# A decoder trunk on one core: the second pass of each feed forward begins with its gate and up column as one pair made of seven products of quarters

## The chip, the core and the metric

The kernel runs on one core of a Trainium2 chip. The core has a matrix engine (PE, with its weight loads shown apart as PEld), a vector engine (DVE), an activation engine (ACT), GpSimd (POOL) and a sync engine (SP) that mostly starts DMAs. The metric is the device time of one execution in microseconds (us), the median of several runs.

## What is computed

A trunk of two layers over 512 tokens of width 1024: a gated DeltaNet mixer in the first, sliding-window attention in the second, both with four heads of attention into memory tokens, and a SwiGLU feed forward behind each mixer. The change touches the feed forwards alone:

```python
D_MODEL, SEQ, D_FF = 1024, 512, 2816

def swiglu(h, w_gate_up, w_down):
    gu = h @ w_gate_up
    return (jax.nn.silu(gu[..., :D_FF]) * gu[..., D_FF:]) @ w_down
...
        x = x + swiglu(rms_norm(x, ln_ffn[layer]), w_gate_up[layer], w_down[layer])
```

## The kernel before, in words

Activations lie with features on the 128 partitions and the 512 tokens along a row. The normed input of a feed forward is eight tiles of 128 features. Every float32 number that goes into a large product is split into a high part (`h`, `whi`) and a low part (`l`, `wlo`), and each product is three matmuls (`mm3`, L198): high by high, high by low, low by high. All go through `mm` and are shown as line L146. The split of a weight tile (`split`, L168) is one copy on ACT (L140, writes `whi`) and one subtraction on DVE (L153, writes `wlo`).

`ffn` (L1099) goes through the 22 column tiles of the hidden width in two passes of 11 (L1167). A pass makes 11 hidden tiles, and then the eight rows of the product with `w_down` add the pass's part to the residual `x`. The rows of the down product have matmuls into the bank `pj`, and their 22 weight splits come in two tiles of 768 and 640 columns for each row.

A column tile of gate or up is made in one of two ways.

- **A whole column** (`projected`, L210): eight tiles of 128 features by three matmuls, 24 matmuls of 128x512. Its weights come in one DMA of 512 KB and are split in one piece of 128x1024.
- **A pair of columns** (`begin`, L1139, with `quarters`, L1275): two columns together, as a product of a 2 by 2 matrix of quarters (which column, which half of the features) with a 2 by 2 matrix of quarters (which half of the features, which half of the tokens). Seven products of quarters stand for the eight, after Strassen and Winograd. Each product is four feature tiles by three matmuls of 128x256, so a pair takes 84 matmuls. On the activations' side the sums of quarters `t1` to `t4` are made once in a feed forward (`token_sums`, tiles `T`). On the weights' side the sums are made for every pair: two by DMAs that add onto a tile that a first DMA has filled (`ws`, L1283 on SP and L1286, L1287 on POOL), two by additions on DVE.

The seven products of a pair stand in this order: `11`, `t1`, `t2`, `21`, `22`, `t3`, `t4`. Three banks with the tag `g` hold them. The first two results are copied out by ACT (`held`, the tiles `fs`), then `t2` goes on top of the first in its bank, and that sum is copied out too. `t4` is the last, and it isn't run at once: `begin` puts it off until the next pair has run its products `11` and `t1`, and at the end of a pass the call of `end` (L1153) releases it.

Split weights of the quarters lie in a ring of six places (`ring`, L1130): three buffers `whi` and three `wlo`, of which each holds two places. Those are the same three buffers that the whole columns and the rows of the down product use. When a pass begins, the ring is laid out anew. The raw weights have two buffers of 1024 columns for whole rows of weights (`wraw`, from the pool of weights) and two of 512 for the last quarter of each pair (`wraw` too, L1289).

A pass begins with a gate and an up column as two whole columns, in both passes, and the other ten columns of gate and of up are pairs (in the first pass two more gate columns are whole, since the sums of tokens are made beside them). So before the change the second pass has two whole columns and ten pairs.

The order of each engine's instructions is set ahead by a scheduler in the framework, which puts DMAs and splits ahead of the code's order where it finds room. Each engine then takes its own list strictly in order (only weight loads overlap matmuls), and waits on semaphores where a row needs another engine's result. SP's and POOL's lists hold the DMA starts.

Of the kernel before, what the change touches and what calls it, by code (L numbers as in the profile page):

```python
# [9 lines left out]
F32 = mybir.dt.float32  # L10
F32R = mybir.dt.float32r
I32 = mybir.dt.int32
AF = mybir.ActivationFunctionType
ALU = mybir.AluOpType
# [4 lines left out]
P = 128  # L19
T = 512  # L20
# [66 lines left out]
class Builder:  # L87
# [1011 lines left out]
    def ffn(self, fp, xp, layer, h, apool, rope=False):  # L1099

        nc, a = self.nc, self.a
        acc = self.acc
        half = FT // 2
        acts, sums, open_pairs, places, waiting, shift, sized = [], [], [], [], [], [0], []

        col = lambda f, up: a["wgu"][layer, 2 * f + up]

        def gate(f, up=()):
            ps = self.project(col(f, 0), h, "pj")
            if f == 0:  # L1110
                list(zip(range(2), up))
                self.rstd_from(acc, *(self.t(fp, [P, T], F32R, "ws", 4) for _ in range(2)), after=self.last,
                               root=(self.cosT, self.sinT) if layer else None)
                self.use(SILU_SIN)
            g = self.t(fp, [P, T], F32, "fg", 4)
            self.tt(nc.vector, g, ps, self.rstd, ALU.mult)
            if f == 2:
                waiting.append(g)
            else:
                self.fn(g, g, AF.Silu)  # L1120
            return g

        def put(u):
            n = len(acts)
            if n == FT // 2 - 1 and not sized:
                sized.append(self.t(fp, [P, 40], F32, "rest"))
            acts.append(self.pair(apool) if n < KD else self.pair(fp, f"ac{n}"))
            self.split(u, *acts[-1])
# [10 lines left out]
        def begin(f, up, by, tag, bufs, then):  # L1139

            o = [self.t(fp, [P, T], F32, tag, bufs) for _ in range(2)]
            steps = self.quarters(fp, [col(f + i, up) for i in range(2)], sums, by, o, ring)
            shift[0] = P - 8
            next(steps)
            while waiting:
                x = waiting.pop()
                self.nosync(self.fn(x, x, AF.Silu), self.held)
            end()
            next(steps)
            open_pairs.append((steps, then, o))  # L1150
            return o

        def end():  # L1153
            if open_pairs:
                steps, then, o = open_pairs.pop()
                next(steps, None)
                for x in o:
                    then(x)

        def add(x, ps):  # L1160
            d = ps
            if not layer:
                d = self.t(fp, [P, T], F32, "fu", 3)
                self.tt(nc.vector, d, ps, self.rstd, ALU.mult)
            self.tt(nc.vector, x, d, x, ALU.add)

        for f0 in (0, half):  # L1167
            acts.clear()
            places.clear()
            up = self.projected(col(f0, 1), h, "g")  # L1170
            g = gate(f0, up)
            u = self.t(fp, [P, T], F32, "fu", 3)
            self.tt(nc.vector, u, list(up)[-1], g, ALU.mult)
            put(u)
            for f in range(f0 + 1, f0 + half, 2):
                if f == 1:
                    g = []
                    for i in range(2):
                        for _ in range(2 - i):
                            sums.append(self.token_sums(fp, layer, len(sums), h))  # L1180
                        g.append(gate(f + i))
                    sums.append(self.token_sums(fp, layer, len(sums), h))
                else:
                    g = begin(f, 0, (self.rstd, self.rstd), "fg", 4, lambda x: self.fn(x, x, AF.Silu))
                begin(f, 1, g, "fu", 3, put)
            end()
            self.acc = self.floor if layer else None
            tail = KD - 2 if f0 and layer else KD
            down = lambda m, j, n, **kw: self.weight(a["wdn"][layer, m][:, (f0 + j) * P:(f0 + j + n) * P], **kw)
            for m in range(tail):  # L1190
                if layer and f0 == 0:
                    self.tt(nc.vector, self.x[m], self.x[m], self.root, ALU.mult)
                ps = self.bank("pj")
                for j, n in ((0, 6), (6, 5)):
                    w = down(m, j, n)
                    for k in range(n):
                        self.mm3(ps, w, k, acts[j + k], j + k == 0, j + k == half - 1)
                add(self.x[m], ps)
                if f0:
                    self.acc = self.accumulate(xp, self.acc, self.x[m], m)  # L1200
                if rope and f0 == 0 and m == 0:
                    self.rope_tables(fp)
        if tail < KD:
# [31 lines left out]
            for n, (end, o) in enumerate(zip(ends, outs)):  # L1235
                self.store(*end, o, n)
# [35 lines left out]
        parts["21"], parts["22"] = ([x[:, i * q:(i + 1) * q] for x in h[j + 4]] for i in range(2))  # L1272
        return parts

    def quarters(self, fp, src, sums, by, u, ring):  # L1275

        nc = self.nc
        q = T // 2
        (a11, a12), (a21, a22) = ([c[:, :T], c[:, T:]] for c in src)
        a1 = self.load(src[0])  # L1280
        s1, s3 = (self.t(fp, [P, T], F32, "ws", 4) for _ in range(2))
        for to, part in ((s1, a21), (s3, a11)):
            ins = nc.sync.dma_start(to, part).ins  # L1283
            if self.behind is not None:
                self.nosync(ins, self.behind)
        nc.gpsimd.dma_start(s1, a22, accum_op=ALU.add)  # L1286
        nc.gpsimd.dma_start(s3, a21, accum_op=ALU.add)  # L1287
        last = self.t(fp, [P, T], F32, "wraw", 2)
        ins = nc.sync.dma_start(last, a22).ins  # L1289
        if self.behind is not None:  # L1290
            self.nosync(ins, self.behind)
        pa, pb, pc = (self.bank("g")[:, :q] for _ in range(3))

        def product(ps, raw, b, first):

            w = ring()
            self.split(raw, *w)
            for j in range(4):
                self.mm3(ps, w, j, sums[j][b], first and j == 0, j == 3, not first)

        def held(ps):
            o = self.t(fp, [P, q], F32, "fs", 3)
            self.copy(o, ps)
            return o

        product(pa, a1[:, :T], "11", True)
        p1 = held(pa)
        self.held = self.copied
        product(pc, s1, "t1", True)
        p5 = held(pc)  # L1310
        yield

        self.tt(nc.vector, a1[:, :T], s1, a1[:, :T], ALU.add)
        product(pa, a1[:, :T], "t2", False)
        u2 = held(pa)
        product(pb, a1[:, T:], "21", True)
        self.tt(nc.vector, u[0][:, :q], pb, p1, ALU.add)
        self.tt(nc.vector, a1[:, T:], a1[:, :T], a1[:, T:], ALU.add)
        product(pc, a1[:, T:], "22", False)
        self.tt(nc.vector, u[0][:, q:], pc, u2, ALU.add)  # L1320
        self.tt(nc.vector, u[0], u[0], by[0], ALU.mult)
        product(pa, s3, "t3", False)
        self.stt(u[1][:, q:], pa, -1.0, p5, ALU.mult, ALU.subtract)
        self.tt(nc.vector, u[1][:, q:], u[1][:, q:], by[1][:, q:], ALU.mult)
        yield
        product(pa, last, "t4", False)
        self.stt(u[1][:, :q], pa, -1.0, by[1][:, :q], ALU.mult, ALU.mult)
# [290 lines left out]
```

## Time and profile before

| | |
|---|---|
| median of 3 runs | 1130.86 us (1130.72 to 1131.07) |
| span of the profiled execution, first to last instruction | 1129.4 us |
| so around that span | about 1.5 us |
| PE / PEld / DVE / ACT / POOL busy | 1119.9 / 986.1 / 827.6 / 634.4 / 73.2 us |
| second pass, layer 0: two whole columns and ten pairs | about 466.7 to 577.0 us |
| second pass, layer 1: the same | about 949.8 to 1060.1 us |

The page gives one time of the profiled execution, its span; the runs' median lies 1.5 us above it, and that is taken as the part outside of the first and last instruction. Times of rows are microseconds from the span's start, a second number is a duration. The chain of waits lists in order of time what the end of the program depended on; a piece such as `x24` is so many instructions one behind another on one engine. A matmul's own duration in a timeline (0.39 us for 128x512) is longer than its distance to the next, because matmuls overlap; the distance is what counts on PE.

### The profile page before, as it was taken

How to read it: one execution, taken by the hardware profiler on the slowest of the kernel's cores; microseconds unless marked ns; L12 is line 12 of the kernel's file. 1: busy time of each engine (PE TensorE's matmuls, PEld its weight loads, DVE VectorE, ACT ScalarE, POOL GpSimd, SP SyncE). 2: the span in 40 equal slices, each digit the busy share in tenths (PEclk: the TensorE clock that was granted, in tenths of full speed). 3: DMA queues.
4: the chain of work that ended last, by engine and by line, in shares of the span. 5: the costliest groups of instructions: out<-in, count | busy, mean ns of one | idle time of the engine just before them, and what ended most of it. 6: DMA issues, size and time to landing. Idle time of an engine off the chain costs nothing.

```text
span 1129.4 us, 19330 instructions
## 1 busy us (share of the span) xinstructions
PE 1119.9 (99%) x7339; PEld 986.1 (87%) x7339; DVE 827.6 (73%) x1553; ACT 634.4 (56%) x1285; POOL 73.2 (6%) x91
## 2 busy tenths in 40 slices
PE   9999999999999999999999999999999999999997
PEld 8888778887899988899988887788999988999986
DVE  7676976577888975588955877839999634889643
ACT  8588664456566632366643555856666422666434
POOL 0000000000021001011000000000111000111001
PEclk9999999999999999999999999999999999999999
DMA  8344252234567536377533321116687533776232
GB/s 314 109 153 149 95 131 86 85 113 145 174 167 195 143 111 169 102 191 195 134 89 102 132 75 38 53 43 180 158 201 185 144 103 105 173 190 156 77 103 87
DMA packets 72401, 151.15 MB, mean 134 GB/s; under 512 B 16956, under 2 KB 18516, under 8 KB 72308
## 3 DMA queue, kind: packets, MB, share of 16 engines
q1 hardware_dynamic: 60884, 129.21, 36.3%
q0 software_dynamic: 11136, 20.45, 11.2%
q8 instruction: 57, 0.93, 0.3%
q14 instruction: 36, 0.29, 0.1%
q10 hardware_dynamic: 288, 0.26, 0.1%
HBM read 142.94 MB, written 6.96 MB: 133 GB/s over the span
## 4 chain that ended last, share of the span: by engine, by line
PE 96%; DVE 2%; ACT 1%; DMA 0%; issue 0%; DVEq 0%; SPq 0%; ACTq 0%
PE pj L146 46%; PE g L146 38%; PE sc L146 6%; PE qk L146 3%; PE pt L146 2%; PE pt L150 1%; PE g L150 1%; DVE big L153 1%; DVE qv L156 0%; DVE btmp L153 0%; DMA early<-in_early 0%; DVE wlo L153 0%; ACT sm L134 0%; DVE T L153 0%; DVE gcr L153 0%
## 5 line engine op out<-in xcount | busy, mean ns | idle before, releaser
L140 ACT ACTIVATE whi<-wraw 128x512 fp32r<-128x512 f32 (+3 forms) x318 | 235.3, 748 | 240.6 <-PE pj L146 164.0
L153 DVE TENSOR_TENSOR wlo<-wraw,whi 128x512 fp32r<-128x512 f32 (+3 forms) x318 | 262.8, 837 | 92.7 <-ACT whi L140 85.2
L146 PE MATMUL pj<-h,whi 128*128 128x512 f32 (+1 forms) x652 | 256.4, 395 | 0.0
L146 PE MATMUL pj<-l,whi 128*128 128x512 f32 (+1 forms) x652 | 254.4, 390 | 0.0
L146 PE MATMUL pj<-h,wlo 128*128 128x512 f32 (+1 forms) x652 | 254.0, 390 | 0.0
L146 PE MATMUL g<-T,whi 128*128 128x256 f32 x1216 | 216.8, 279 | 0.0
L146 PEld LDWEIGHTS g<-T,whi 128*128 128x128 f32 x1216 | 185.1, 188 | 1.3 <-DVE fu L156 1.3
L146 PE MATMUL g<-T,wlo 128*128 128x256 f32 x608 | 169.7, 279 | 0.0
L146 PEld LDWEIGHTS pj<-h,whi 128*128 128x128 f32 x652 | 122.4, 188 | 28.0 <-issue 4.1
L146 PEld LDWEIGHTS pj<-h,wlo 128*128 128x128 f32 x652 | 122.5, 188 | 25.4 <-issue 0.9
L146 PE MATMUL g<-l,whi 128*128 128x256 f32 (+1 forms) x500 | 144.5, 289 | 0.0
L146 PE MATMUL g<-h,whi 128*128 128x256 f32 (+1 forms) x500 | 144.4, 289 | 0.0
L146 PE MATMUL g<-h,wlo 128*128 128x256 f32 (+1 forms) x500 | 144.4, 289 | 0.0
L146 PEld LDWEIGHTS pj<-l,whi 128*128 128x128 f32 x652 | 122.6, 188 | 23.6 <-DVE l L1468 0.3
L146 PEld LDWEIGHTS g<-T,wlo 128*128 128x128 f32 x608 | 114.3, 188 | 0.0
L146 PEld LDWEIGHTS g<-h,whi 128*128 128x128 f32 x500 | 94.0, 188 | 1.9
L146 PEld LDWEIGHTS g<-l,whi 128*128 128x128 f32 x500 | 93.9, 188 | 1.9
L146 PEld LDWEIGHTS g<-h,wlo 128*128 128x128 f32 x500 | 93.9, 188 | 1.8
L1286 POOL DMA_DIRECT2D ws<-in_wgu x38 | 33.5, 881 | 733.0 <-DMA ws<-in_wgu 399.1
L140 ACT ACTIVATE whi<-ws 128x512 fp32r<-128x512 f32 x76 | 48.0, 631 | 42.0 <-PE g L146 35.6
L153 DVE TENSOR_TENSOR wlo<-ws,whi 128x512 fp32r<-128x512 f32 x76 | 52.0, 684 | 5.9 <-ACT whi L140 5.9
L1287 POOL DMA_DIRECT2D ws<-in_wgu x38 | 34.2, 900 | 196.4 <-DVE wlo L153 71.4
(421 smaller groups left out, 1683.2 us busy)
## 6 DMA issues: line engine op xcount, KB each, us to landing
wraw<-in_wgu SPq DMA_DIRECT2D x50, 512.0 KB, 4.4
ws<-in_wgu SPq DMA_DIRECT2D x76, 256.0 KB, 3.4
ws<-in_wgu POOLq DMA_DIRECT2D x76, 256.0 KB, 4.5
wraw<-in_win SPq DMA_DIRECT2D x26, 512.0 KB, 3.6
wraw<-in_wdn SPq DMA_DIRECT2D x32, 384.0 KB, 3.1
wraw<-in_wdn SPq DMA_DIRECT2D x32, 320.0 KB, 2.9
wraw<-in_wgu SPq DMA_DIRECT2D x38, 256.0 KB, 4.0
wraw<-in_wout SPq DMA_DIRECT2D x16, 512.0 KB, 3.6
```

The lines of the kernel that those rows point to most:

```text
L140: self.copied = self.nc.scalar.activation(out, in_, AF.Copy, **kw).ins
L146: return self.nc.tensor.matmul(out, lhsT, rhs, start=start, stop=stop, skip_group_check=more).ins
L150: return self.nc.tensor.transpose(out, in_, self.ident[:k, :k]).ins
L153: return eng.tensor_tensor(out=out, in0=a, in1=b, op=op).ins
L1286: nc.gpsimd.dma_start(s1, a22, accum_op=ALU.add)
L1287: nc.gpsimd.dma_start(s3, a21, accum_op=ALU.add)
```

## The change

The first gate column and the first up column of the second pass are no longer two whole columns. A new function `both` takes them as one pair through `quarters`: the pair's first column is the gate, its second the up column. The gate half is scaled by `rstd` as before and goes through SiLU in the middle of the pair (`then`), and the up half is multiplied by it. The first pass stays as it was.

```diff
+        def both(f):
+
+            o = [self.t(fp, [P, T], F32, *kind) for kind in (("fg", 4), ("fu", 3))]
+            steps = self.quarters(fp, [col(f, up) for up in range(2)], sums, (self.rstd, o[0]), o, ring,
+                                  lambda: self.fn(o[0], o[0], AF.Silu))
+            next(steps)
+            next(steps)
+            open_pairs.append((steps, put, o[1:]))
+
...
         for f0 in (0, half):
             acts.clear()
             places.clear()
-            up = self.projected(col(f0, 1), h, "g")
-            g = gate(f0, up)
-            u = self.t(fp, [P, T], F32, "fu", 3)
-            self.tt(nc.vector, u, list(up)[-1], g, ALU.mult)
-            put(u)
+            if f0:
+                both(f0)
+            else:
+                up = self.projected(col(f0, 1), h, "g")
+                g = gate(f0, up)
+                u = self.t(fp, [P, T], F32, "fu", 3)
+                self.tt(nc.vector, u, list(up)[-1], g, ALU.mult)
+                put(u)
...
-    def quarters(self, fp, src, sums, by, u, ring):
+    def quarters(self, fp, src, sums, by, u, ring, then=None):
...
         self.tt(nc.vector, u[0], u[0], by[0], ALU.mult)
+        if then is not None:
+            then()
         product(pa, s3, "t3", False)
```

In the lists of the engines this moves rows at two places of each second pass. The first is ACT's list where the first pass's down product ends and the second pass begins, in layer 0. `whi_839` is the last weight tile of the down product, `wraw_842` and `wraw_848` are the two whole columns, `wraw_856` the first pair. Before:

```order
L140 ACTIVATE whi_839_4876<-wraw_838_4874 128x640
L140 ACTIVATE whi_843_4900<-wraw_842_4898 128x1024
L140 ACTIVATE whi_849_4935<-wraw_848_4933 128x1024
L140 ACTIVATE whi_863_4984<-wraw_856_4971 128x512
L140 ACTIVATE whi_863_4984<-ws_857_4973 128x512
L140 ACTIVATE whi_865_4986<-wraw_856_4971 128x512 x2
L134 ACTIVATE fg_846_4929<-fg_846_4929 128x512
L140 ACTIVATE whi_867_4988<-wraw_856_4971 128x512
L140 ACTIVATE whi_867_4988<-ws_858_4974 128x512
L140 ACTIVATE h_852_4965<-fu_847_4932 128x512
L140 ACTIVATE whi_863_4984<-wraw_874_5089 128x512
L140 ACTIVATE fs_869_5004<-g_860_4981 128x256
```

And in the changed kernel, where `wraw_844`, `ws_845` and `ws_846` are the new pair and `wraw_862` is the pair behind it:

```order
L140 ACTIVATE whi_839_4876<-wraw_838_4874 128x640
L140 ACTIVATE whi_851_4913<-wraw_844_4900 128x512
L140 ACTIVATE whi_851_4913<-ws_845_4902 128x512
L140 ACTIVATE whi_853_4915<-wraw_844_4900 128x512 x2
L140 ACTIVATE whi_855_4917<-wraw_844_4900 128x512
L140 ACTIVATE whi_855_4917<-ws_846_4903 128x512
L140 ACTIVATE whi_851_4913<-wraw_862_5019 128x512
L140 ACTIVATE fs_857_4933<-g_848_4910 128x256
L140 ACTIVATE whi_851_4913<-ws_863_5021 128x512
```

The two copies of 128x1024 are gone, and the copies for six products of the new pair stand in one row behind the down product's last; the first copy out of a bank (`fs_857`) stands behind the first copy for the next pair (`whi_851` from `wraw_862`).

The second place is the end of the second pass. On PE, in layer 0, `pj` is the first row of the down product and `g` from `T_612` on is the last pair's put-off product `t4`. Before:

```order
L146 MATMUL g_990_6155<-T_637_3272,wlo_866_4987 128x256
L146 MATMUL pj_1000_6295<-h_852_4965,whi_1002_6298 128x512
L146 MATMUL pj_1000_6295<-l_853_4966,whi_1002_6298 128x512
L146 MATMUL pj_1000_6295<-h_852_4965,wlo_1003_6299 128x512
L146 MATMUL pj_1000_6295<-h_895_5278,whi_1002_6298 128x512
L146 MATMUL pj_1000_6295<-l_896_5279,whi_1002_6298 128x512
L146 MATMUL g_990_6155<-T_612_3163,whi_865_4986 128x256
```

And in the changed kernel:

```order
L146 MATMUL g_992_6216<-T_637_3272,wlo_854_4916 128x256
L146 MATMUL pj_1002_6356<-h_871_5079,whi_1004_6359 128x512
L146 MATMUL pj_1002_6356<-l_872_5080,whi_1004_6359 128x512
L146 MATMUL pj_1002_6356<-h_871_5079,wlo_1005_6360 128x512
L146 MATMUL g_992_6216<-T_612_3163,whi_855_4917 128x256
```

Two matmuls of the down product stood ahead of `t4` and now stand behind it: `t4` has three ahead of it in place of five.

DVE's list at that same point, from the first weight tile of the down product on. `fu` from a bank `g` and a tile `fs` is the reading of the bank behind product `t3`. Before:

```order
L153 TENSOR_TENSOR wlo_1003_6299<-wraw_1001_6296,whi_1002_6298 128x768
L153 TENSOR_TENSOR fu_984_6143<-g_992_6157,fs_995_6222 128x256
L153 TENSOR_TENSOR fu_984_6143<-fu_984_6143,fg_968_6008 128x512
L153 TENSOR_TENSOR wlo_1006_6323<-wraw_1004_6320,whi_1005_6322 128x640
L156 SCALAR_TENSOR_TENSOR fu_985_6144<-g_990_6155,fs_994_6188 128x256
```

And in the changed kernel:

```order
L153 TENSOR_TENSOR wlo_1005_6360<-wraw_1003_6357,whi_1004_6359 128x768
L153 TENSOR_TENSOR fu_986_6204<-g_994_6218,fs_997_6283 128x256
L153 TENSOR_TENSOR fu_986_6204<-fu_986_6204,fg_970_6069 128x512
L156 SCALAR_TENSOR_TENSOR fu_987_6205<-g_992_6216,fs_996_6249 128x256
L153 TENSOR_TENSOR fu_987_6205<-fu_987_6205,fg_971_6070 128x256
L153 TENSOR_TENSOR wlo_1008_6384<-wraw_1006_6381,whi_1007_6383 128x640
```

The subtraction for the down product's second weight tile (128x640) stood ahead of the reading of the bank and now stands two rows behind it. Both places look the same in layer 1.

## The prediction

> **What bounds the kernel now.** I read the page first: busy time, granted clock, and the chain that ended last.
>
> ```profile
> PE 1119.9 (99%) x7339; PEld 986.1 (87%) x7339; DVE 827.6 (73%) x1553; ACT 634.4 (56%) x1285; POOL 73.2 (6%) x91
> PEclk9999999999999999999999999999999999999999
> PE 96%; DVE 2%; ACT 1%; DMA 0%; issue 0%; DVEq 0%; SPq 0%; ACTq 0%
> ```
>
> PE is on the chain for 96% of the span, at full clock. So the question is whether PE has gaps where the change works. For that I took the chain in the two stretches of the second passes, layer 0 and then layer 1.
>
> ```profile
> 472.16 102.05 PE g L146 x852
> 574.21 1.16 PE pj L146 x5
> 575.37 1.67 PE g L146 x12
> 577.04 2.99 PE pj L146 x13
> ...
> 955.21 102.05 PE g L146 x852
> 1057.26 1.16 PE pj L146 x5
> 1058.42 1.66 PE g L146 x12
> 1060.08 4.99 PE pj L146 x22
> ```
>
> Nothing but PE stands there: a second pass is as long as its matmuls, with a possible exception where the last product of the last pair (the 12 matmuls into `g`) is fitted in between rows of the down product. The distances between matmuls come from two pure pieces of the whole chain, and the end of the first pass serves for comparison.
>
> ```profile
> 269.05 5.44 PE g L146 x24
> ...
> 801.60 86.80 PE g L146 x744
> ...
> 405.33 0.69 PE pj L146 x3
> 406.02 1.49 PE g L146 x12
> 407.51 1.62 PE pj L146 x7
> ```
>
> A whole column is 24 matmuls of 128x512 in 5.44 us, 0.2267 us each. The 744 are all quarters of 128x256 in a first pass: 86.80/744 = 0.1167 us. The second pass agrees: 102.05 less one whole column (5.44) over 828 quarters is 0.1167.
>
> **The change part by part.**
>
> *Matmuls.* Each second pass loses two whole columns, 2 x 5.44 = 10.88 us, and gains a pair, 84 x 0.1167 = 9.80 us: **1.08 us less** in each of two passes, if PE is fed. Whole columns and pairs lie on the path, so this counts in full. The bounds of this term are narrow, since both distances are read from hundreds of equal rows.
>
> The Trainium skill ("TensorE: Matmul & The Clock Gate", section "Back-to-back issue gap") speaks against more and smaller matmuls: each pays a fixed issue cost, 518 cycles for 512 columns and 262 for 256 at 2.4 GHz, isolated. By that a pass would go from 48 x 215.8 to 84 x 109.2 ns, 1.19 us less, an estimate from that page, and the whole sum would come to 1128.1. The rows show 226.7 and 116.7 ns, both longer than the page's, and the rows decide.
>
> *The end of the second pass.* PE from 574.21 to 577.04 takes 2.83 us for five matmuls of `pj` and the twelve of `t4`. Without two of the `pj` (0.45) that is 2.38. At the end of the first pass three `pj` and twelve `g` take 407.51 - 405.33 = 2.18. So the second pass loses 0.20 us there (1057.26 to 1060.08 gives 0.19). The reason stands in these rows: PE and DVE, second pass, then the same at the end of the first.
>
> ```profile
> 574.97 0.40 PE L146 MATMUL pj<-l,whi 128*128 128x512 f32 x1
> 575.35 0.51 PE L146 MATMUL g<-T,whi 128*128 128x256 f32 x2
> ...
> 574.14 0.82 DVE L153 TENSOR_TENSOR wlo<-wraw,whi 128x640 fp32r<-128x640 f32 x1
> 574.88 0.42 DVE L156 SCALAR_TENSOR_TENSOR fu<-g,fs 128x256 f32<-128x256 f32 x1
> ...
> 405.63 0.39 PE L146 MATMUL pj<-h,wlo 128*128 128x512 f32 x1
> 405.86 0.48 PE L146 MATMUL g<-T,whi 128*128 128x256 f32 x2
> ...
> 405.37 0.42 DVE L156 SCALAR_TENSOR_TENSOR fu<-g,fs 128x256 f32<-128x256 f32 x1
> 406.17 0.82 DVE L153 TENSOR_TENSOR wlo<-wraw,whi 128x640 fp32r<-128x640 f32 x1
> ```
>
> `t4` adds onto a bank that DVE reads first. In the second pass DVE does the 128x640 subtraction ahead of that reading, which ends at 575.30, and `t4` starts 0.38 behind the matmul before it in place of 0.23. In the first pass the reading comes first and ends at 405.79, as the third `pj` is through. The changed lists have the first pass's order at the second pass's end, on DVE and on PE alike. So I take **0.19 us less** a pass. Bounds: at best 0.20 comes back; at worst the gap stays, or grows by the two matmuls that moved behind `t4` (0.45 us a pass).
>
> *Splits and additions on ACT and DVE.* A pair needs more of them than two whole columns:
>
> ```profile
> L140 ACT ACTIVATE whi<-wraw 128x512 fp32r<-128x512 f32 x190 | 116.8, 627 | 63.1 <-PE g L146 41.7 <-PE pj L146 14.3 <-DVE wraw L153 3.2
> L153 DVE TENSOR_TENSOR wlo<-wraw,whi 128x512 fp32r<-128x512 f32 x190 | 127.6, 688 | 16.9 <-ACT whi L140 12.1
> L140 ACT ACTIVATE whi<-wraw 128x1024 fp32r<-128x1024 f32 x66 | 69.3, 1054 | 46.2 <-PE pj L146 42.8 <-DMA wraw<-in_wout 2.6 <-DVE wlo L153 0.4
> L153 DVE TENSOR_TENSOR wlo<-wraw,whi 128x1024 fp32r<-128x1024 f32 x66 | 80.0, 1218 | 25.3 <-ACT whi L140 22.7 <-PE pj L146 2.5
> ...
> 466.50:477.30 10.80, 10.80 (x49) 8.93 (x49) 5.68 (x9) 2.83 (x5) 0.87 (x1) 1.00 0.37 96
> 477.60:487.40 9.80, 9.80 (x87) 9.80 (x86) 8.91 (x16) 6.05 (x13) 1.74 (x2) 1.00 0.59 162
> ```
>
> The last two rows are windows: length, then busy PE, PEld, DVE, ACT, POOL. ACT loses 2 x 1.05 and gains 7 x 0.63 and three copies out of banks. DVE loses 2 x 1.22 and gains 7 x 0.69, and a pair's additions and readings. What that comes to is the second window, one pair of the steady run: DVE 8.91 of 9.80 us, ACT 6.05, and PE without a gap. I cost it at **nothing**: the pair's own matmuls hide it. DMA share goes from 0.37 to 0.59 there and POOL gets two DMA starts more, in a stretch where both have room. If the cover failed, DVE has under 0.9 us a pair to catch up with.
>
> What is new is the place: nothing but the down product comes ahead of the pair now. Its ring buffers are those of the down product.
>
> ```profile
> 459.05 1.06 ACT L140 ACTIVATE whi<-wraw 128x1024 fp32r<-128x1024 f32 x1 [2.66 <-PE pj L146]
> 463.13 1.06 ACT L140 ACTIVATE whi<-wraw 128x1024 fp32r<-128x1024 f32 x1 [3.02 <-PE pj L146]
> 466.53 0.63 ACT L140 ACTIVATE whi<-wraw 128x512 fp32r<-128x512 f32 x1 [2.34 <-PE pj L146]
> ```
>
> These are the moments at which PE gives the three buffers free; the down product ends at about 466.6. The new pair puts products one and two in the first, three and four in the second, five and six in the third. A product is 12 x 0.1167 = 1.40 us. One and two are split by about 462, three and four by about 465.5. Five and six can only start at 466.53: ACT 2 x 0.63, on DVE two rows of 0.69 for `x7` and two for the splits, ready by about 468.1 and 469.3. PE wants them at 466.6 + 4 x 1.40 = 472.2 and at 473.6. So 4 us are to spare, and I take **no stall**; the bound is one pass of a split from ACT through DVE to PE, 0.63 + 0.69 = 1.3 us a pass, and nothing below zero, since PE isn't seen to wait at this seam now.
>
> *A wait that is added.* The copy `fs_857` of the first product must be out before `t2`. On ACT it stands behind the copy of the next pair's first quarter, which needs a DMA and product one's end. This is how pairs run now:
>
> ```profile
> 457.28 4.91 SPq L179 DMA_DIRECT2D wraw<-in_wgu  x2
> ...
> 479.04 0.62 ACT L140 ACTIVATE whi<-wraw 128x512 fp32r<-128x512 f32 x1
> 479.56 0.36 ACT L140 ACTIVATE fs<-g 128x256 f32<-128x256 f32 x1
> ...
> wraw<-in_wgu SPq DMA_DIRECT2D x50, 512.0 KB, 4.4
> ...
> 441.96 0.87 POOL L1287 DMA_DIRECT2D ws<-in_wgu  x1 [7.45 <-DMA ws<-in_wgu]
> ```
>
> On SP's list the next pair's load takes the place of the up column's, issued at 457.28, 4.4 to land: there by 461.7, wanted at 466.6 + 1.40 = 468.0. Behind it on ACT stand the copies out of banks, and PE waits for those. With 6 us to spare it costs nothing. The additions by DMA keep their order on SP and POOL; the last of the first two pairs' four starts at 441.96, 25 us ahead of the pass.
>
> **The sum**: 2 x (1.08 + 0.19) = 2.54 us. The span goes from 1129.4 to 1126.9; with the 1.5 us around it, 1130.86 - 2.54 = **1128.3**. A difference that the measurement tells from none is about 0.2%, 2.26 us, so the bound lies at 1128.6, close to the forecast.
>
> **The rivals.** One row of ACT's timeline at the second pass's end bears on the first of them.
>
> ```profile
> 569.76 1.28 ACT L125 ACT_TABLE_LOAD   x1
> ```
>
> - *The end of the pass gains nothing.* ACT loads a table in the second pass's end and not in the first's, so the first pass's order might not give its timing. Only the matmuls count: 1130.86 - 2.16 = 1128.7. Against it: the reading of the bank is DVE's, and its order is now the first pass's; the table is loaded 4 us ahead (569.76 + 1.28).
> - *The beginning starves.* Five and six come late by the 1.3 us of one split, in each pass: 2.54 - 2.6, 1130.9. Against it: the 4 us worked out above.
> - *Slower: ACT's queue is stuck behind a load.* If the next pair's first load isn't there when product one ends, `fs_857` and `t2` wait behind it. It costs from a landing time of 4.4 + 6.8 = 11.2 us on (468.0 plus some 0.4 that `t1` leaves, less 457.28). For 0.2% slower than before the two passes must wait (2.54 + 2.26)/2 = 2.4 us each, a landing of 13.6 us, three times the median: 1133.1.
> - *A quarter isn't nearly half.* Equal cost is at 10.88/84 = 0.1295 us a matmul. At three quarters of a whole one, 0.170 us, a pass takes 14.28, 3.40 more: 1137.3. The 0.1167 of all pairs speak against it. The Trainium skill gives in that same section a sustained 131 ns at 512 columns and 81 at 128 with weight loads, on a straight line some 98 at 256, an estimate of just that ratio; the whole columns' 226.7 ns here don't agree with it.
>
> That the change doesn't do what it says is out: PE's list has 72 rows more, twice 84 less 48.
>
> **How the numbers follow.** The forecast has 0.64, the end without gain 0.18, the starved beginning 0.11, the stuck queue 0.05, the dear quarter 0.02. Forecast and first rival lie on either side of 1128.6 by 0.3 and 0.1 us; what each loses over the bound by noise I take as even. So faster 0.64, same 0.29, slower 0.07. The range takes in the forecast, 0.5 us below it for what the runs scatter and for gaps that I don't see, the first rival, and stalls of up to about half a us a pass: 1127.8 to 1129.4.
>
> **What would show it.** The second passes' chain should read as one piece of `g` of some 912 quarters at 0.1167, straight behind the down product's last `pj`, with no other engine in it, and 9.80 us in place of 10.88. At its end three `pj`, then `t4` in about 1.49. The reading of the bank should end within 0.7 us of `t3`. It is wrong if PE shows idle time behind ACT or DVE within 10 us of the down product's end, if `fs` starts later than 0.6 us behind product one, or if `t4` starts more than 0.25 us behind the `pj` ahead of it.

## The result and the profile after

| | before | changed |
|---|---|---|
| median of 21 runs each | 1130.86 us (1130.41 to 1132.49) | 1129.5 us (1129.12 to 1131.18) |
| ratio | | 0.9987, 95% interval 0.9981 to 0.9993 |
| span of the profiled execution | 1129.4 us | 1127.8 us |
| PE / DVE / ACT busy | 1119.9 / 827.6 / 634.4 us | 1117.4 / 837.6 / 640.9 us |

The change gains 1.4 us, a little over half of the 2.54 forecast. The gain is real, since the interval leaves out 1, but at 0.13% it falls under the 0.2% that was to count as faster. The 1129.5 stand 1.2 us above the forecast, and 0.1 us above the end of its range.

The page of the changed kernel, its busy times, the clock, and one group of matmuls (busy time and mean, then the idle time ahead of it and who ended it):

```profile
PE 1117.4 (99%) x7411; PEld 987.9 (88%) x7411; DVE 837.6 (74%) x1575; ACT 640.9 (57%) x1301; POOL 76.6 (7%) x95
PEclk9999999999999999999999999999999999999999
...
L146 PE MATMUL pj<-h,whi 128*128 128x512 f32 (+1 forms) x636 | 250.5, 396 | 1.1 <-DVE fu L153 1.1
```

The last row is the first hint. The same group on the page of before:

```profile
L146 PE MATMUL pj<-h,whi 128*128 128x512 f32 (+1 forms) x652 | 256.4, 395 | 0.0
```

Before, this group had 0.0 us of idle time; now it has 1.1, all behind one operation of DVE.

The second passes themselves came out as forecast. The chain of waits in order of time (start, us, what), layer 0 and then layer 1:

```profile
466.36 106.40 PE g L146 x912
572.76 0.69 PE pj L146 x3
573.46 1.50 PE g L146 x12
574.95 51.48 PE pj L146 x227
...
949.52 106.40 PE g L146 x912
1055.92 0.69 PE pj L146 x3
1056.61 1.49 PE g L146 x12
1058.10 52.16 PE pj L146 x261
```

A pass begins with one piece of 912 quarters, 106.40/912 = 0.1167 us each, and no other engine stands in it. It ends with three `pj` and then `t4` in 1.49 to 1.50 us. From the last-but-one product to the first row behind `t4` it takes 574.95 - 572.76 = 2.19 us, where the first pass took 2.18. The windows of the new pair and of the next one (busy PE, PEld, DVE, ACT, POOL, clock, DMA share, GB/s) show that the extra splits are hidden:

```profile
466.50:476.30 9.80, 9.80 (x86) 9.80 (x86) 8.96 (x16) 5.64 (x12) 1.77 (x2) 1.00 0.66 173
476.30:486.10 9.80, 9.80 (x86) 9.80 (x86) 8.93 (x17) 6.26 (x13) 1.74 (x2) 1.00 0.86 201
```

PE has no gap in either. The loss lies 60 us further on, where layer 0's second down product ends and the queries of layer 1's attention begin. The chain of the changed kernel there:

```profile
626.51 1.06 ACT whi L140
...
632.41 2.07 DVE l L156 x3
634.49 0.61 DVE fu L153
635.10 0.14 issue
635.23 7.09 PE pj L146 x30
```

Before, the chain had a single piece at this place:

```profile
577.04 65.59 PE pj L146 x289
```

PE's timeline of the changed kernel, with the last two matmuls of the down product and the first two of the first query (start, duration, what; in brackets the idle time ahead):

```profile
633.51 0.39 PE L146 MATMUL pj<-ac10l,whi 128*128 128x512 f32 x1
633.74 0.39 PE L146 MATMUL pj<-ac10h,wlo 128*128 128x512 f32 x1
635.23 0.47 PE L146 MATMUL pj<-h,whi 128*128 128x512 f32 x1 [1.10 <-DVE fu L153]
635.54 0.39 PE L146 MATMUL pj<-l,whi 128*128 128x512 f32 x1
```

From start to start that is 1.49 us where 0.23 is usual, so 1.27 us are lost. (The 1.10 in brackets counts from the modelled end of the matmul ahead.) The other side of it on DVE, in the changed kernel and then before:

```profile
630.43 4.06 DVE L156 SCALAR_TENSOR_TENSOR l<-x,gains,h 128x512 fp32r<-128x512 f32 x6
634.40 0.69 DVE L153 TENSOR_TENSOR fu<-pj,rstd 128x512 f32<-128x512 f32 x1
```

```profile
632.09 4.06 DVE L156 SCALAR_TENSOR_TENSOR l<-x,gains,h 128x512 fp32r<-128x512 f32 x6
636.06 0.68 DVE L153 TENSOR_TENSOR fu<-pj,rstd 128x512 f32<-128x512 f32 x1
```

`fu<-pj,rstd` is the row in `add` that reads the last down row out of its bank. DVE did nothing different: the same six subtractions stood ahead of the reading before, and it was as late. PE didn't wait for it then, as its timeline of before shows, with the last down matmul and the first query's first:

```profile
635.40 0.39 PE L146 MATMUL pj<-ac10h,wlo 128*128 128x512 f32 x1
635.63 0.39 PE L146 MATMUL pj<-h,whi 128*128 128x512 f32 x1
```

That query began 0.43 us ahead of the reading (636.06). What is new is that PE waits. The balance of the trace: 2 x 1.27 less in the passes, 1.27 more at this place, and the profiled execution came 0.34 us earlier to the first feed forward (318.03 in place of 318.37 for its first quarter), which is scatter. Together that is 1.61 us less; the spans differ by 1.6. (That a pass gains as much as this place loses is chance.)

**The theory.** Down rows and queries write banks (pieces of the memory that matmuls write into) with the tag `pj`, of which there are two, taken in turn. Before, layer 0's second pass took nine of them, one for the whole gate column and eight for the down rows; now it takes eight. The attention's queries begin a new turn with the first bank. In the addresses of the two programs:

```
                              before   changed
last down row but one         bank 0   bank 1
last down row                 bank 1   bank 0
first query of the attention  bank 0   bank 0
```

Before, the first query took the bank that DVE had read 7 us earlier (from 628.35 on); now it takes the bank of the row that has just ended. **The rival**: the first query waits for ScalarE's copy of its weights; ACT's rows stand in the chain there too. The view of waits of the changed kernel between 625 and 640 us lists, for PE and its weight loads:

```profile
PEld pj L146 <- ACT whi L140: 1.5, 1, 1.5
...
PE pj L146 <- DVE fu L153: 1.1, 1, 1.1
```

Both theories have a row there, so the view alone doesn't decide.

### The profile page after: what moved, and what is told of

The parts are those of the page before. It is cut to its first block, busy times and chain, and to the rows that moved or that the text cites. A ratio compares the mean times of both kernels' runs of the same rounds, so it can differ in the third digit from the quotient of the medians.

```text
span 1127.8 us, 19543 instructions
## 1 busy us (share of the span) xinstructions
PE 1117.4 (99%) x7411; PEld 987.9 (88%) x7411; DVE 837.6 (74%) x1575; ACT 640.9 (57%) x1301; POOL 76.6 (7%) x95
## 4 chain that ended last, share of the span: by engine, by line
PE 95%; DVE 2%; ACT 1%; DMA 0%; issue 0%; DVEq 0%; SPq 0%; ACTq 0%
PE pj L146 44%; PE g L146 39%; PE sc L146 6%; PE qk L146 3%; PE pt L146 2%; PE pt L150 1%; PE g L150 1%; DVE big L153 1%; DVE qv L156 0%; DVE btmp L153 0%; ACT h L140 0%; DVE wlo L153 0%; DMA early<-in_early 0%; ACT sm L134 0%; ACT whi L140 0%
## 5 line engine op out<-in xcount | busy, mean ns | idle before, releaser
L146 PE MATMUL pj<-h,whi 128*128 128x512 f32 (+1 forms) x636 | 250.5, 396 | 1.1 <-DVE fu L153 1.1
L146 PE MATMUL pj<-l,whi 128*128 128x512 f32 (+1 forms) x636 | 248.4, 391 | 0.0
L146 PE MATMUL pj<-h,wlo 128*128 128x512 f32 (+1 forms) x636 | 248.0, 391 | 0.0
L146 PE MATMUL g<-T,whi 128*128 128x256 f32 x1280 | 228.1, 280 | 0.0
L146 PEld LDWEIGHTS g<-T,whi 128*128 128x128 f32 x1280 | 194.9, 188 | 1.0 <-DVE fu L156 1.0
L146 PE MATMUL g<-T,wlo 128*128 128x256 f32 x640 | 178.9, 279 | 0.0
L146 PEld LDWEIGHTS pj<-h,whi 128*128 128x128 f32 x636 | 119.5, 188 | 28.7 <-issue 4.1
L146 PEld LDWEIGHTS pj<-h,wlo 128*128 128x128 f32 x636 | 119.6, 188 | 24.8 <-issue 0.9
L146 PEld LDWEIGHTS g<-T,wlo 128*128 128x128 f32 x640 | 120.4, 188 | 0.0
L1298 POOL DMA_DIRECT2D ws<-in_wgu x40 | 36.0, 901 | 726.8 <-DMA ws<-in_wgu 293.8
L1299 POOL DMA_DIRECT2D ws<-in_wgu x40 | 35.8, 895 | 198.3 <-DVE wlo L153 80.8
```

The source lines that it names most:

```text
L146: return self.nc.tensor.matmul(out, lhsT, rhs, start=start, stop=stop, skip_group_check=more).ins
```

## The experiments

The first four ran on one chip, beside 29 runs of the kernel before (1131.06 us). The others had one run each beside one of the kernel before, so for them the traces decide and not the times.

**e1: the bank taken back.** The changed kernel, and the new pair of layer 0 takes one of its three banks from `pj`, so that a second pass takes nine again. Each engine's instructions stand in the same order as in the changed kernel.

```diff
-                                  lambda: self.fn(o[0], o[0], AF.Silu))
+                                  lambda: self.fn(o[0], o[0], AF.Silu), "g" if layer else "pj")
...
-        pa, pb, pc = (self.bank("g")[:, :q] for _ in range(3))
+        pa, pb, pc = (self.bank(n)[:, :q] for n in ("g", tag, "g"))
```

> The changed kernel, but in layer 0 the new pair holds its product 21 in a bank of the tag pj in place of g. Every engine has the same rows in the same order; only the banks alternate so that the last row of layer 0's down product and the first query behind it are again in different banks. Theory (PE waits 1.27 us in front of the first query because that query's bank is the one that DVE hasn't read yet): the gap of 1.49 us between two matmuls at 633.74 goes to about 0.25, span 1126.4 to 1126.6, ratio to before about 0.9976 to 0.9979. Rival (PE waits there for ACT's copy of a weight tile, or DVE is simply late at that place): the gap stays at 1.4 to 1.5 us, span 1127.8, ratio 0.9987.

Measured: 1128.23 us (1127.95 to 1128.53), ratio 0.9973 (0.9963 to 0.9984). PE's and DVE's timelines at the seam:

```profile
633.53 0.39 PE L146 MATMUL pj<-ac10h,wlo 128*128 128x512 f32 x1
633.76 0.39 PE L146 MATMUL pj<-h,whi 128*128 128x512 f32 x1
```

```profile
634.20 0.68 DVE L153 TENSOR_TENSOR fu<-pj,rstd 128x512 f32<-128x512 f32 x1
```

The reading is still late, and the first query starts 0.44 us ahead of it, 0.23 behind the last down matmul. The gap is gone with nothing changed but which banks the products take. This kernel is faster than both others, though the changed one's 1129.5 comes from other runs, with 1130.86 for the kernel before in place of 1131.06.

**e2: the shift alone.** The kernel before, without the pair. The up column of layer 0's second pass takes its bank from `pj` in place of `g`, so that this pass takes ten and the turn is swapped as in the changed kernel.

```diff
-            up = self.projected(col(f0, 1), h, "g")
+            up = self.projected(col(f0, 1), h, "g" if layer or not f0 else "pj")
```

> The kernel before, but in layer 0's second pass the whole up column goes into a bank of the tag pj in place of g, so the banks alternate as in the changed kernel; no instruction more or less. Theory (the bank is the cause): a gap of about 1.5 us between the last matmul of layer 0's down product and the first query, span 1129.4 + 1.3 = 1130.7, ratio to before 1.0011. Rival (the loss comes from the pair, not from the bank): no gap, ratio 1.000.

Measured: 1132.71 us (1131.96 to 1137.06), ratio 1.0019 (1.001 to 1.0029). PE's timeline at the seam:

```profile
634.76 0.39 PE L146 MATMUL pj<-ac10h,wlo 128*128 128x512 f32 x1
636.25 0.47 PE L146 MATMUL pj<-h,whi 128*128 128x512 f32 x1 [1.10 <-DVE fu L153]
```

The same gap of 1.49 us, in a kernel that has none of the change. The median rose by 1.65 us, more than the gap's 1.27; the runs of this kernel scatter up to 1137.06, and what they lose besides wasn't followed.

**e3 and e4: one layer alone.** The pair in the second pass of layer 1 only, then of layer 0 only.

```diff
-            if f0:
+            if f0 and layer:
```

```diff
-            if f0:
+            if f0 and not layer:
```

> The change in layer 1's second pass alone; layer 0 begins its second pass with two whole columns as before. Theory (each pass gains 1.08 in matmuls and 0.19 at its end, and the loss sits in layer 0 alone): 1.27 us less than before, span 1128.1, ratio 0.9989, and no gap behind layer 0's down product. Rival (each pass gains half of what was forecast): 0.7 us less, ratio 0.9994.

> The change in layer 0's second pass alone. Theory: 1.27 us gained in the pass and 1.3 us lost in front of the first query, so span and time as before within 0.2 us, ratio 1.0000; layer 0's second pass itself reads 1.27 us shorter. Rival (each pass gains half): ratio 0.9994 and no gap.

Measured: e3 1129.23 us (1129.01 to 1129.93), ratio 0.9983 (0.9974 to 0.9992); e4 1130.91 us (1130.4 to 1131.15), ratio 0.9996 (0.9988 to 1.0005). The chain at the seam, of e3 and then of e4:

```profile
576.98 65.59 PE pj L146 x289
```

```profile
574.99 51.52 PE pj L146 x227
...
634.55 0.61 DVE fu L153
635.16 0.14 issue
635.29 7.07 PE pj L146 x30
```

Layer 1's pair gains by itself all that the change gained, and has no gap. Layer 0's pair gives back behind its pass what it gains in it. For e4 the time alone would allow the rival too (0.9994 lies in its interval); the gap decides.

**e5: the reading brought forward.** The changed kernel, with four of the six subtractions ordered behind the reading.

```diff
-                self.tt(nc.vector, d, ps, self.rstd, ALU.mult)
+                self.read = self.tt(nc.vector, d, ps, self.rstd, ALU.mult)
...
                 self.split_gain(self.x[k], self.gain(base, k), *t[k])
+                if t is h and 3 <= k < 7:
+                    self.nosync(self.low, self.read)
```

> The changed kernel with VectorE's reading of layer 0's last down row ordered ahead of four of the six subtractions l<-x,gains,h that stand before it at the end of layer 0's second feed forward. Theory (the first attention query waits for the end of that reading, because it takes the same bank): the matmul of the first query still starts about 0.14 us behind the end of the reading, and the gap between the last down matmul and the first query (1.49 us from start to start in the changed kernel) falls to 1.0 to 1.2 us, since VectorE's subtractions of 0.68 us each no longer all stand ahead. Rival (the first query waits for ScalarE's copy of its first weights): the gap stays at 1.49 us however early the reading ends.

Measured: 1132.93 us in the one run (before 1131.1 beside it). The gap did not fall; it grew to 2.21 us. DVE, then PE:

```profile
633.29 0.75 DVE L156 SCALAR_TENSOR_TENSOR l<-x,gains,h 128x512 fp32r<-128x512 f32 x1 [1.21 <-ACT h L140]
634.24 1.23 DVE L153 TENSOR_TENSOR wlo<-wraw,whi 128x1024 fp32r<-128x1024 f32 x1 [0.20 <-ACT whi L140]
635.38 0.68 DVE L153 TENSOR_TENSOR fu<-pj,rstd 128x512 f32<-128x512 f32 x1
```

```profile
634.00 0.39 PE L146 MATMUL pj<-ac10h,wlo 128*128 128x512 f32 x1
636.21 0.47 PE L146 MATMUL pj<-h,whi 128*128 128x512 f32 x1 [1.82 <-DVE fu L153]
```

The scheduler put a weight subtraction of 1.23 us and another `l` ahead of the reading in place of the four, so it came later, not earlier. The number expected was wrong in sign, but the point at issue is answered: the query moved with the reading and starts 0.15 behind its end (635.38 + 0.68), while the rival had the gap stay at 1.49.

**e7: the same, with those two rows held back as well.**

```diff
-                if t is h and 3 <= k < 7:
+                if (3 if t is h else 6) <= k < 7:
                     self.nosync(self.low, self.read)
...
+            if t == 7:
+                self.nosync(self.low, self.read)
```

> The run e5_read_first pushed a 128x1024 weight subtraction and another l<-x,gains,h ahead of the reading that it was to bring forward; here both are ordered behind it, so that only subtractions whose inputs are early stand ahead. Theory (the query waits for VectorE's reading of the shared bank): with VectorE free, a reading starts 0.43 us behind the start of its row's last matmul (626.26 to 626.69 in the changed kernel), takes 0.61 to 0.69 and the query starts 0.14 behind it, so the gap is 1.18 to 1.26 us: 0.25 us or so of the 1.49 are VectorE's queue, the rest is the price of sharing the bank. Rival (ScalarE's weights): 1.49 as before.

Measured: 1130.72 us in one run (before 1131.29 beside it). DVE, then PE:

```profile
634.43 0.69 DVE L153 TENSOR_TENSOR fu<-pj,rstd 128x512 f32<-128x512 f32 x1 [2.34 <-PE pj L146]
```

```profile
634.00 0.39 PE L146 MATMUL pj<-ac10h,wlo 128*128 128x512 f32 x1
635.26 0.47 PE L146 MATMUL pj<-h,whi 128*128 128x512 f32 x1 [0.88 <-DVE fu L153]
```

DVE now waits for PE. The reading starts 0.43 us behind the start of the row's last matmul and takes 0.69, and the query starts 0.14 behind its end. The gap is 1.26 us. So of the 1.27 us lost in the changed kernel only 0.23 were DVE's queue, and 1.04 are the price of sharing a bank with the row ahead: the end of the row, the reading, and the way back to PE. A DVE that stands ready doesn't take that away; another bank does (e1). The kernel as a whole gains nothing by e7: the weight subtraction that was held back now makes PE pause for 1.13 us from start to start at 641.0.

**e5 once more.** In e5's profile, seven matmuls behind the gap stood 0.43 us apart, and the window there showed a clock of 0.50. Whether a gap of this length brings that about was asked by running the same kernel again.

> The kernel of e5_read_first once more, unchanged. In its one profile seven matmuls behind the gap of 2.21 us stood 0.43 us apart instead of 0.23, at a granted clock of 0.50, and then the clock was full again. If a gap of that length costs the clock, this run shows the same stretch at 0.5 again behind a gap of 2.2 us; if that was a chance event of one execution, the matmuls stand 0.23 apart.

Measured: 1130.35 us in one run (before 1131.29 beside it). The window 638 to 640 us, of e5 and then of its repetition (columns as above):

```profile
638.00:640.00 2.00, 2.00 (x6) 1.52 (x5) 2.00 (x4) 1.85 (x3) 0.00 (x0) 0.50 0.83 305
```

```profile
638.00:640.00 2.00, 2.00 (x10) 1.67 (x9) 2.00 (x4) 1.77 (x3) 0.00 (x0) 1.00 0.80 291
```

The gap was there again, the low clock was not. PE in the repetition:

```profile
633.91 0.39 PE L146 MATMUL pj<-ac10h,wlo 128*128 128x512 f32 x1
636.12 0.47 PE L146 MATMUL pj<-h,whi 128*128 128x512 f32 x1 [1.83 <-DVE fu L153]
```

So the 1.6 us that e5 lost by the low clock belong to one execution. So do some 0.8 more in layer 1's first pass, where its 744 quarters took 87.61 us in place of 86.80, at a clock of 1.00 throughout; the reason wasn't found. Its 1132.93 isn't the cost of the edit.

**e6: the end of the pass alone.** The kernel before, with one order changed: DVE reads the put-off product's bank ahead of the 128x640 subtraction.

```diff
+                    if f0 and m == 0 and j:
+                        self.nosync(self.low, self.read)
...
-        self.stt(u[1][:, q:], pa, -1.0, p5, ALU.mult, ALU.subtract)
+        self.read = self.stt(u[1][:, q:], pa, -1.0, p5, ALU.mult, ALU.subtract)
```

> The kernel before with one order changed: at the end of each second pass VectorE reads the bank of the put-off product ahead of the 128x640 subtraction for the next column's weights. Theory of the prediction's second term (the put-off product loses its time to that reading): the end of the pass shows three down products and then t4, the matmuls from the last-but-one product to the first down row behind it take about 2.19 us as in the first pass, 0.19 us less for each second pass, and there is no gap ahead of the first attention query, since the banks alternate as before; the time falls by 0.4 us, to about 1130.5. Rival (the loss at the end comes from elsewhere, say ScalarE's table or the weights): t4 still starts some 0.2 us late and the passes are as long as before.

Measured: 1131.28 us in one run (before 1131.1 beside it); 0.4 us can't be seen in one run against one. The trace can show it. The chain at the end of layer 0's pass:

```profile
574.32 0.69 PE pj L146 x3
575.01 1.49 PE g L146 x12
576.50 66.04 PE pj L146 x291
```

Three `pj` and `t4` take 2.18 us, where the kernel before took 2.83 with two `pj` more (0.45), so 0.20 less; and there is no gap at the seam, where nine banks are taken. Layer 1's end takes 2.18 as well (1057.22 to 1059.40). The second term's mechanism is shown by itself.

How the cases add up, from the start of the first quarter of the first feed forward to the start of the last matmul in each profile, which leaves out the scatter ahead of it:

```
before                  803.17
changed                 802.01   -1.16
e1 bank taken back      800.65   -2.52
e2 shift alone          804.63   +1.46
e3 layer 1 only         802.05   -1.12
e4 layer 0 only         803.27   +0.10
e5 read first           805.19   +2.02
e5 once more            802.65   -0.52
e7 read clean           802.96   -0.21
e6 end of the pass      802.89   -0.28
```

The forecast of 2.54 less is what e1 shows. Layer 0's pair with its gap (e4) is worth nothing, and layer 1's alone (e3) is worth the whole change. The changed kernel and e1 differ by 1.36 us here and not by 1.27: the 30 matmuls behind the gap take 7.09 us in the changed kernel, and the same 30 take 7.01 in e1.

## Why the prediction came out half right

- **Matmuls, 1.08 us a pass: right.** 912 quarters at 0.1167 us stand where 24 matmuls of a gate, 24 of an up column and 828 quarters stood. Both passes came out with the time forecast. The price that was weighed there from the Trainium skill ("TensorE: Matmul & The Clock Gate", section "Back-to-back issue gap"), 262 cycles (109.2 ns) for 256 columns, is again shorter than the row (116.7 ns).
- **The end of the pass, 0.19 us: right, and its reason as well.** 2.19 us after the change; e6 gets 2.18 with the order of DVE's rows alone. The first rival, in which the end gains nothing, is out, although by its time (1128.7) it lies nearer to the result than the forecast.
- **Splits, additions and the added wait at nothing: right.** PE stands without a gap in the new pair and behind it, DVE is busy for 8.96 of 9.80 us against 8.91 forecast. The starved beginning (1130.9) is out, and neither the stuck queue nor the dear quarter came.
- **The sum: wrong, for want of a term.** "The sum: 2 x (1.08 + 0.19) = 2.54 us" counted what the edit does to instructions, and stopped at the pass's end. The list of what goes away with a whole column had its matmuls, its DMA and its splits, and not its bank. That one `pj` less turned the alternation round for layer 0's last down row, and the first query, which always begins with the first bank, ran into it: 1.27 us more, once. The Trainium skill ("Perfetto Trace Analysis", section "Optimizing Tensor Performance") advises that independent groups of matmuls take PSUM banks in turn, so that the reading of one lies beside the next one's matmuls. Within a stage these rows do so, with no wait in the trace; where one stage's turn ends and the next one's begins, the two kernels differ by the 1.27 us. With the term the sum is 2.54 - 1.27 = 1.27, or 1129.6 by the prediction's own arithmetic; 1129.5 was measured. That the result came so near to the range's end is luck: the room there was for stalls in each pass, and no pass had one.
- **Why none of its tests caught it.** They looked for idle time within 10 us of the first down product's end and at the end of the pass. The lateness of DVE's reading could be read in the profile of before, 0.43 us behind the first query's start. It was harmless there for one reason only, the other bank.
- **The chances.** Faster by over 0.2% had 0.64, and the result lies within 0.2%, which had 0.29. The forecast stood only 0.3 us beyond that bound, so that a single unseen gap of 0.3 us was enough.

Why layer 1 pays nothing: its second pass took eleven `pj` banks before, one for the whole column, six for down rows and four for the last two rows, which are made in halves. Now it takes ten. By the addresses the turn is swapped there too, but the two banks still alternate from row to row, and no stage behind it begins a new turn: the kernel's last products go into `g`. In e3's trace PE waits for no engine from 1050 us to the end.

## What to carry to other kernels

When an edit takes away or adds a tile from a pool that is used in turn, count the tiles that each stage takes, before and after, and look at the next stage's first use: an odd difference turns two banks round, and a late reading that cost nothing becomes a wait. The candidates can be found in the profile of before: readings of a bank that end behind the start of the next product in the other bank. If one of them turns out to be exposed, giving it the other bank back (1.27 us here) is worth more than making the reader earlier (0.23 us).

## What the runs showed of the hardware

In one of two executions of the same kernel (e5), the granted clock fell to 0.50 for some 3.4 us behind a gap of 2.21 us on PE (by windows of one us, 0.83 from 636 to 637, 0.50 up to 640, 0.96 up to 641) and cost 1.6 us (the 30 matmuls behind the gap took 8.69 us in place of 7.05); in the other, behind a gap of 2.22, it stayed at 1.00. The gaps of 1.49 us showed full clock in the three profiles that had them (the changed kernel, e2, e4). The Trainium skill ("TensorE: Matmul & The Clock Gate", section "What's actually happening") says that the clock is halved after an idle window of about 3.4 us; a gap of 2.2 us is shorter than that, and one execution showed the halved clock all the same. What decides between the two executions is open.
